# Two-layer hybrid trunk on one core: half of a strided gather moved from ScalarE to GpSimd, a deeper first load queue, new hand orders

## The chip, the cores and the metric

The kernel runs on one core of a Trainium2 chip. The metric is device time in microseconds (us). TensorE (PE) multiplies matrices, VectorE (DVE), ScalarE (ACT) and GpSimd (POOL) work elementwise, and SyncE (SP) issues the DMA loads. Each engine runs its own instructions in program order and waits on semaphores for the others.

## The reference

Two layers over x of 256 tokens by 1024 channels, all float32. Each layer has a token mixing and a feed-forward part, both behind an RMS norm whose scale, shift and gate come from a vector c through `w_mod` (the "modulation"):

```
mod = silu(c) @ w_mod[l] + b_mod[l]                  # 6 x 1024 numbers
h   = rms_norm(x, norm1) * (1 + scale1) + shift1
proj = h @ w_in                                      # u (512) | q (512) | 3 x k,v (768) | gates (24)
y_pool = mean of u over windows of 2, 4, 8, 16 tokens, minus u, times pool_w, per group of 128 channels
k_cmp, v_cmp = silu(flatten(32-token blocks, stride 16) @ cmp_w1) @ cmp_w2      # 15 blocks
y_nsa = gated sum of compressed, selected and sliding-window attention (q, k normed and rotated)
x = x + gate1 * (concat(y_pool, y_nsa) @ w_out)
h2 = rms_norm(x, norm2) * (1 + scale2) + shift2
x = x + gate2 * (relu(h2 @ w_ff1)**2 @ w_ff2)
```

## The kernel before

**Layout and precision.** x stays in on-chip memory transposed, 128 partitions by 8 chunks by 256 tokens. Most products are done as three matmuls of split operands: a value is `hi` (rounded) plus `lo` (the rest), and `mm3` (L269) issues hi·hi, hi·lo and lo·hi (L274 to L276). A few products run in plain float32 (L272, L686).

**The stream of weights.** All weights come as one list of tiles of 512 KB (`stream`, L164 to L190), loaded in list order by SP. `load` (L206) issues loads as long as fewer than six tiles lie between the oldest one in use and the newest. `step` (L220) takes the next tile: a "mod" tile goes to one multiply-accumulate on VectorE (L231), which gives one column of the modulation; any other is split, hi by a cast on ScalarE (L237), lo by a subtraction on VectorE (L238), into five buffers of each kind. `pump` (L242) takes as many tiles as its limits allow. The pool of raw tiles has six buffers; those for hi and lo lie idle while the first 24 tiles pass, since these are used as they come (mod, mod, a for each of eight chunks).

**Stages.** 0 to 46 us: the start and layer 0's first projection, chunk by chunk (L674 to L689: two modulation columns, `modulate` with `mt` L427 and `n` L433, then 12 matmuls L686). 46 to about 134 us: layer 0's token mixing. To 315 us: its feed-forward. 315 to about 427 us: layer 1's token mixing. To 608 us: its feed-forward, then the output.

**The order of the mixing.** Each layer's mixing is written as a string of items (`ORDER`), each the name of a closure with numbers: `b,n,..` and `a,c,h` are pieces of the projection (TensorE), `mod,k` is one normalised chunk (ScalarE h L430, VectorE `mt` L427 and h L431), `nl,n` normalises a finished projection tile (VectorE L641, ScalarE L642), `gather,kv` and `comp` the compression, `psums,g` and `pmix,g` the pooling (GpSimd L590 to L594, VectorE L598), `squares`, `rotate`, `sum`, `turn` the norm and rotation of q and k, `pump,m,n` takes stream tiles. The items are issued in that order, and a scheduler then orders every engine's instructions again; the result stands in the order rows below.

**The compression.** The k and v tiles `kvT` are copied by `gather` (L520) into `tb`, eight copies of 64 partitions by 16 by 15 elements that read every sixteenth token; 64 narrow matmuls `ph` (L533) follow, and the rest of the projection stands behind them on TensorE.

**Rotation.** `squares` (L736) gives sums of squares `ss`, GpSimd raises them to the power -1/2 (`rs`, L751), `rotate` (L753) multiplies the projection in its PSUM bank by the tables (`x` L761, two `z` L764) and by that releases the bank, `rotate_sum` (L766) adds and scales.

**Feed-forward.** In layer 1 the first `EARLY_FF` blocks of 128 features are computed from the chunks before the norm's factor is known; the factor is applied to their results (`act`, L972: b copy L980, r L981), and `TURNS` says how many of the eight chunks are normalised (`modulate`) after each block; the blocks after the early ones read these. `NORM_AT` says at which matmul the two halves of the norm's factor are issued, `WARM` how many dummy matmuls (L307) stand at four places of the start, `MODS` after which tile of layer 0's mixing how many of its mod tiles stand in the stream.

Of the kernel before, what the change touches and what calls it, by code (L numbers as in the profile page):

```python
# [10 lines left out]
F32 = mybir.dt.float32  # L11
F32R = mybir.dt.float32r
# [5 lines left out]
L, D, S, P = 2, 1024, 256, 128  # L18
# [9 lines left out]
WARM = (14, 2, 6, 4)  # L28
# [5 lines left out]
EARLY_FF = (8, 11)  # L34
# [3 lines left out]
NORM_AT = ((1, 2), (2, 7), (1, 2), (1, 6))  # L38

TURNS = ((0, 0, 2, 3, 2, 1, 0, 0, 0, 0), (0, 0, 1, 1, 2, 1, 1, 1, 1, 0))  # L40
# [5 lines left out]
MODS = (0, 0, 2, 5, 0, 2, 2, 5, 4, 0, 0, 1, 1, 2)  # L46

ORDER = (
# [79 lines left out]
def raw(ap):  # L128
    return ap.bitcast(F32)
# [3 lines left out]
def trunk(ctx: ExitStack, tc: tile.TileContext, ins, out):  # L133
# [66 lines left out]
    def source(b):  # L200
        w = ins["w_" + b[0] + ("0" if b[:2] == ("a", 0) else "")]
        for i in b[1:]:
            w = w[i]
        return w, (NA if b[0] == "a" else D)

    def load():  # L206
        nonlocal loaded
        while loaded < min(len(stream), min([used] + held) + N_RAW):
# [940 lines left out]
```

## Time and profile before

| | |
|---|---|
| median of 3 runs | 613.72 us (613.46 to 614.18) |
| the profiled execution | 613.58 us, its span 611.8 us, mean granted TensorE clock 0.994 |
| busy | PE 594.2 us, DVE 469.3, ACT 354.8, POOL 72.4 |
| DMA | 147.5 MB, 241 GB/s over the span |

The span is what the trace covers; the remaining 1.8 us lie around it. Busy times are sums over the whole span, so PE is idle in it for 17.6 us; where they lie is a question for the waits and the windows. A row of a timeline has the start, the duration of that line's run of like instructions, engine, line, tile written and tiles read, the count, and in brackets the idle time of the engine before it with what released it.

### The profile page before, as it was taken

How to read it: one execution, taken by the hardware profiler on the slowest of the kernel's cores; microseconds unless marked ns; L12 is line 12 of the kernel's file. 1: busy time of each engine (PE TensorE's matmuls, PEld its weight loads, DVE VectorE, ACT ScalarE, POOL GpSimd, SP SyncE). 2: the span in 40 equal slices, each digit the busy share in tenths (PEclk: the TensorE clock that was granted, in tenths of full speed). 3: DMA queues.
4: the chain of work that ended last, by engine and by line, in shares of the span. 5: the costliest groups of instructions: out<-in, count | busy, mean ns of one | idle time of the engine just before them, and what ended most of it. 6: DMA issues, size and time to landing. Idle time of an engine off the chain costs nothing.

```text
span 611.8 us, 12176 instructions
## 1 busy us (share of the span) xinstructions
PE 594.2 (97%) x4676; PEld 550.3 (90%) x4676; DVE 469.3 (77%) x870; ACT 354.8 (58%) x781; POOL 72.4 (12%) x94
## 2 busy tenths in 40 slices
PE   8899899999999999999998989999999999999997
PEld 5558767789999999999998978788999999999997
DVE  5769999899999888988876979858996765444440
ACT  3125766478777763443447767866887777433330
POOL 1013630040000000010033640003000000000000
PEclk9999999999999999999998989999999999999999
DMA  8999857965799999998993443233667776666600
GB/s 336 368 386 335 320 186 248 335 215 195 263 363 378 333 332 369 321 366 276 388 359 128 149 139 104 70 100 114 204 222 256 232 234 192 186 204 196 196 30 18
DMA packets 40856, 147.51 MB, mean 241 GB/s; under 512 B 4543, under 2 KB 5725, under 8 KB 40541
## 3 DMA queue, kind: packets, MB, share of 16 engines
q1 hardware_dynamic: 40653, 146.20, 69.3%
q8 instruction: 37, 0.61, 0.4%
q10 hardware_dynamic: 144, 0.52, 0.3%
q14 instruction: 22, 0.18, 0.1%
HBM read 145.66 MB, written 1.05 MB: 240 GB/s over the span
## 4 chain that ended last, share of the span: by engine, by line
PE 80%; DVE 8%; DMA 4%; ACT 4%; POOL 2%; issue 2%; ACTq 0%; DVEq 0%
PE pg L275 10%; PE pg L276 10%; PE pg L274 10%; PE pf L275 10%; PE pf L276 10%; PE pf L274 10%; DMA w<-in_w_mod 3%; PE pb L272 2%; PE pout L272 2%; PE po L898 2%; PE pt L879 2%; DVE w L231 2%; DVE h L443 1%; DVE lo L238 1%; PE pa L686 1%
## 5 line engine op out<-in xcount | busy, mean ns | idle before, releaser
L238 DVE TENSOR_TENSOR lo<-w,hi 128x1024 fp32r<-128x1024 f32 (+1 forms) x154 | 189.4, 1234 | 68.7 <-ACT hi L237 68.1
L237 ACT CAST hi<-w 128x1024 fp32r<-128x1024 f32 (+1 forms) x154 | 160.8, 1049 | 127.7 <-PE pg L275 57.9
L275 PE MATMUL pf<-h,hi 128*128 128x256 f32 (+1 forms) x512 | 145.2, 284 | 1.9 <-DVE h L443 1.9
L274 PE MATMUL pf<-h,hi 128*128 128x256 f32 (+1 forms) x512 | 144.3, 283 | 0.0
L276 PE MATMUL pf<-h,lo 128*128 128x256 f32 (+1 forms) x512 | 144.2, 282 | 0.0
L276 PE MATMUL pg<-a,lo 128*128 128x256 f32 x512 | 144.1, 281 | 0.0
L274 PE MATMUL pg<-a,hi 128*128 128x256 f32 x512 | 143.7, 281 | 0.0
L275 PE MATMUL pg<-a,hi 128*128 128x256 f32 x512 | 143.6, 280 | 0.0
L231 DVE SCALAR_TENSOR_TENSOR w<-w,cb 128x1024 f32<-128x1024 f32 x96 | 119.3, 1249 | 10.7 <-DMA w<-in_w_mod 10.0
L275 PEld LDWEIGHTS pf<-h,hi 128*128 128x128 f32 x512 | 96.8, 189 | 3.4 <-DVE h L443 3.4
L276 PEld LDWEIGHTS pf<-h,lo 128*128 128x128 f32 x512 | 96.9, 189 | 0.0
L274 PEld LDWEIGHTS pg<-a,hi 128*128 128x128 f32 x512 | 96.7, 189 | 0.0
L274 PEld LDWEIGHTS pf<-h,hi 128*128 128x128 f32 x512 | 96.5, 189 | 0.1
L275 PEld LDWEIGHTS pg<-a,hi 128*128 128x128 f32 x512 | 96.3, 188 | 0.0
L276 PEld LDWEIGHTS pg<-a,lo 128*128 128x128 f32 x512 | 96.2, 188 | 0.0
L686 PE MATMUL pa<-w,n 128*128 128x280 f32 (+2 forms) x96 | 29.8, 463 | 2.9 <-ACT n L433 2.5
L686 PEld LDWEIGHTS pa<-w,n 128*128 128x128 f32 x96 | 17.7, 190 | 15.0 <-issue 8.3
L274 PE MATMUL pout<-h,hi 128*128 128x256 f32 x96 | 28.0, 296 | 0.4 <-DVE xT L930 0.4
L856 ACT ACTIVATE p<-sc,nm 128x128 f32<-128x128 f32 (+1 forms) x64 | 26.1, 423 | 2.8 <-DVE nm L852 2.3
L985 ACT ACTIVATE r<-r 128x256 f32<-128x256 f32 x64 | 26.3, 415 | 1.4
L1038 DVE SCALAR_TENSOR_TENSOR xT<-pg,mod,xT 128x256 f32<-128x256 f32 x16 | 7.7, 484 | 25.1 <-PE pg L276 25.1
L989 DVE TENSOR_TENSOR a<-r,a 128x256 fp32r<-128x256 f32 x64 | 26.6, 420 | 0.5 <-ACT a L986 0.5
(195 smaller groups left out, 936.6 us busy)
## 6 DMA issues: line engine op xcount, KB each, us to landing
w<-in_w_ff SPq DMA_DIRECT2D x128, 512.0 KB, 4.5
w<-in_w_mod SPq DMA_DIRECT2D x96, 512.0 KB, 5.3
w<-in_w_a SPq DMA_DIRECT2D x16, 524.0 KB, 6.6
w<-in_w_out SPq DMA_DIRECT2D x16, 512.0 KB, 4.3
w<-in_w_b SPq DMA_DIRECT2D x12, 512.0 KB, 6.0
lw<-in_lw SPq DMA_DIRECT2D x2, 1360.0 KB, 9.8
out<-xT SPq DMA_DIRECT2D x8, 128.0 KB, 2.8
late<-in_late SPq DMA_DIRECT2D x1, 899.0 KB, 8.2
```

What stands on the lines that cost most here:

```text
L231: V.scalar_tensor_tensor(w[:, :D], w[:, :D], 1.0, cb, op0=ALU.mult, op1=ALU.mult, accum_out=mod[:, b[1], b[2]:b[2] + 1])
L237: A.copy(hi[:, :n], w[:, :n])
L238: (G if by_pool(*b) else V).tensor_tensor(lo[:, :n], w[:, :n], raw(hi[:, :n]), op=ALU.subtract)
L272: T.matmul(o, lhs[0], rhs[0], start=start, stop=stop)
L274: T.matmul(o, lhs[0], rhs[0], start=start, stop=False)
L275: T.matmul(o, lhs[0], rhs[1], start=False, stop=False)
L276: T.matmul(o, lhs[1], rhs[0], start=False, stop=stop)
L686: T.matmul(pa[t, g][:, :n], N1[:, k, t * P:(t + 1) * P], w[:, c0:c0 + n], start=k == 0, stop=k == KD - 1)
L856: A.activation(p[:, e, b], sc[:, e, b], AF.Exp, bias=nm[:, e, b:b + 1], accum_out=self.sums[:, hd, b:b + 1])
L879: T.transpose(pt[:, c * P:(c + 1) * P], p[:, c * P:(c + 1) * P], ident)
L985: A.activation(w, w, AF.Square)
L989: V.tensor_tensor(aT[1][:, f], ws.pop(f), raw(aT[0][:, f]), op=ALU.subtract)
```

## The change

1. In layer 1, `gather` of the second half (kv = 1) goes to GpSimd: four of its eight copies.
2. The first 24 loads may lie in sixteen buffers: six raw, five hi, five lo. From the 25th on the six raw ones serve as before.
3. Both `ORDER` strings are new. Layer 1's has a new item `warm,3` (three dummy matmuls) ahead of `mod,7`. Some flags that say whether ScalarE or VectorE does a scaling differ.
4. `WARM`, `EARLY_FF`, `NORM_AT`, `TURNS` and `MODS` have new numbers.

```diff
-WARM = (14, 2, 6, 4)
+WARM = (14, 1, 9, 2)
-EARLY_FF = (8, 11)
+EARLY_FF = (8, 9)
-NORM_AT = ((1, 2), (2, 7), (1, 2), (1, 6))
+NORM_AT = ((1, 3), (2, 7), (0, 5), (1, 6))
-TURNS = ((0, 0, 2, 3, 2, 1, 0, 0, 0, 0), (0, 0, 1, 1, 2, 1, 1, 1, 1, 0))
+TURNS = ((0, 0, 2, 3, 2, 1, 0, 0, 0, 0), (0, 0, 0, 1, 3, 1, 0, 0, 3, 0))
-MODS = (0, 0, 2, 5, 0, 2, 2, 5, 4, 0, 0, 1, 1, 2)
+MODS = (0, 0, 2, 5, 0, 2, 2, 5, 6, 0, 0, 1, 0, 1)
...
-    "pump,0,2 tables norm,0 b,4,0,7 b,4,7,8 pump,1,4 b,5,0,7 b,5,7,8 keep,5 keep,4 norm,1 mod,0 nl,4 nl,5 b,3,0,8 "
+    "pump,1,1 tables b,4,0,7 pump,2,5 norm,0 b,4,7,8 b,5,0,7 b,5,7,8 keep,4 norm,1 keep,5 nl,4 nl,5 pump,2,4 "
...
+    homes, slots, n_first = {}, {}, 3 * KD
+    for i in range(len(stream)):
+        r = i % (N_RAW + 2 * N_SPLIT)
+        homes[i] = "raw" if i >= n_first or r < N_RAW else "hi" if r < N_RAW + N_SPLIT else "lo"
+        slots.setdefault(homes[i], []).append(i)
+
+    def room(i):
+
+        at = slots[homes[i]]
+        n = at.index(i) - (N_RAW if homes[i] == "raw" else N_SPLIT)
+        return n < 0 or at[n] < used and at[n] not in held
...
-        while loaded < min(len(stream), min([used] + held) + N_RAW):
+        while loaded < len(stream) and room(loaded):
...
-            tiles[loaded] = wraw.tile([P, NA], F32, tag="raw", name="w")
+            if homes[loaded] == "raw":
+                tiles[loaded] = wraw.tile([P, NA], F32, tag="raw", name="w")
+            else:
+                tiles[loaded] = raw(wsp.tile([P, NA], F32R, tag=homes[loaded], name=homes[loaded]))
...
-                        A.copy(tb[par * HD:(par + 1) * HD, :, kv, 15 * g:15 * g + 15], src)
+                        to = tb[par * HD:(par + 1) * HD, :, kv, 15 * g:15 * g + 15]
+                        if kv and not first:
+                            G.tensor_copy(to, src)
+                        else:
+                            A.copy(to, src)
```

In the changed kernel the lines behind `ORDER` are one higher, those behind `load` 17 and those behind `gather` 21 higher than before: L237 is L254, L238 is L255, L430 is L447, L525 is L544 (GpSimd) and L546 (ScalarE), L642 is L663, L750 is L771, L761 is L782, L764 is L785, L769 is L790.

**The gather on ScalarE, layer 1, before.** `rb` is the norm's factor, `kvT` the k and v tiles, `tb` the gathered ones, `u` the pooling input.

```order
L400 COPY rb<-pr 128x256
L237 CAST hi<-w 128x1048
L430 ACTIVATE h_1247<-mt,mod 128x256
L642 ACTIVATE kvT<-nl,early 128x256 x2
L525 COPY tb<-kvT 64x16x15 x8
L642 ACTIVATE u<-nl,bsh 128x256
L430 ACTIVATE h_1247<-mt,mod 128x256
L237 CAST hi<-w 128x1048 x2
```

**The same place after.**

```order
L417 COPY rb<-pr 128x256
L254 CAST hi<-w 128x1048
L663 ACTIVATE kvT<-nl,early 128x256 x2
L447 ACTIVATE h_1258<-mt,mod 128x256
L546 COPY tb<-kvT 64x16x15 x4
L254 CAST hi<-w 128x1048
L663 ACTIVATE u<-nl,bsh 128x256
L447 ACTIVATE h_1258<-mt,mod 128x256
L254 CAST hi<-w 128x1048
```

Four of the eight copies are gone from this row; one h now stands behind `kvT` instead of ahead of it, and the cast that followed `u` and an h stands ahead of them.

**GpSimd at that place, after.** `win` are the pooling sums, made from `u`.

```order
L576 TENSOR_TENSOR ck<-cmpc 30x128
L406 TENSOR_TENSOR r<-v,mhalf 128x2
L544 COPY tb<-kvT 64x16x15 x4
L611 TENSOR_TENSOR win<-u 128x271
L611 TENSOR_TENSOR win<-win 128x269
```

The four copies stand where, before, `win<-u` followed `r` directly.

**Rotation on VectorE, layer 1, before.** `x` and `z` read a projection bank `pa`; the second row of two `z` ends the use of the half bank; `ss` is the sum of squares for GpSimd.

```order
L238 TENSOR_TENSOR lo<-w,hi 128x1048 x2
L761 TENSOR_TENSOR x<-pa,ca 128x256
L750 TENSOR_SCALAR ss<-ss 128x4
L764 TENSOR_TENSOR z<-pa,sb 128x4x32 x2
L761 TENSOR_TENSOR x<-pa,ca 128x256
```

**The same place after**, from the first rotation of the layer on.

```order
L782 TENSOR_TENSOR x<-pa,ca 128x256
L785 TENSOR_TENSOR z<-pa,sb 128x4x32 x2
L255 TENSOR_TENSOR lo<-w,hi 128x1048
L790 TENSOR_TENSOR x<-x,z 128x256
L782 TENSOR_TENSOR x<-pa,ca 128x256
L785 TENSOR_TENSOR z<-pa,sb 128x4x32
L255 TENSOR_TENSOR lo<-w,hi 128x1048
L785 TENSOR_TENSOR z<-pa,sb 128x4x32
L790 TENSOR_TENSOR x<-x,z 128x256
L771 TENSOR_SCALAR ss<-ss 128x4
L782 TENSOR_TENSOR x<-pa,ca 128x256
L785 TENSOR_TENSOR z<-pa,sb 128x4x32 x2
```

Before, `ss` stood between the second rotation's `x` and its two `z`. After, both `z` of that rotation stand ahead of this `ss`, with one weight split between them, and the third rotation stands behind it.

## Rows read from the trace of the kernel before

**Rows 1.** the longest waits of TensorE: line, releaser, us in total, times, longest

```profile
PE pa L274 <- DVE z L764: 2.8, 1, 2.8
PE pa L686 <- ACT n L433: 2.5, 3, 1.3
PE pf L275 <- DVE h L443: 1.9, 6, 0.7
PE ph L533 <- ACT tb L525: 1.6, 1, 1.6
```

**Rows 2.** layer-1 mixing by 15 us: length, busy per engine, PEclk, DMA share, GB/s

```profile
330.00:345.00 15.00, 15.00 (x155) 14.43 (x156) 14.09 (x27) 10.84 (x23) 9.00 (x12) 0.89 0.33 107
345.00:360.00 15.00, 12.21 (x91) 11.39 (x90) 11.73 (x31) 8.49 (x40) 11.10 (x11) 0.98 0.43 141
360.00:375.00 15.00, 14.90 (x113) 14.02 (x113) 13.72 (x40) 11.40 (x40) 3.39 (x3) 0.91 0.42 129
```

**Rows 3.** chain from 8 to 46 us: start, duration, what

```profile
18.13 7.46 DMA w<-in_w_mod
```

**Rows 4.** three 15 us windows of layer 0

```profile
15.00:30.00 15.00, 13.42 (x46) 8.15 (x45) 10.76 (x25) 2.03 (x4) 0.00 (x0) 1.00 1.00 373
60.00:75.00 15.00, 13.94 (x139) 11.19 (x138) 13.72 (x37) 11.30 (x54) 9.32 (x13) 1.00 0.88 327
120.00:135.00 15.00, 13.59 (x108) 12.75 (x106) 14.77 (x26) 9.84 (x20) 6.74 (x7) 1.00 0.66 234
```

**Rows 5.** page part 5, the layer-0 projection: busy, mean ns, idle before

```profile
L686 PE MATMUL pa<-w,n 128*128 128x280 f32 (+2 forms) x96 | 29.8, 463 | 2.9 <-ACT n L433 2.5
```

**Rows 6.** ScalarE in order of time: start, us, instruction, [idle <-releaser]

```profile
324.32 0.90 ACT L642 ACTIVATE kvT<-nl,early 128x256 f32<-128x256 f32 x2
325.12 4.83 ACT L525 COPY tb<-kvT 64x240 f32<-64x240 f32 x8
...
355.55 1.06 ACT L772 ACTIVATE x<-x,rs 128x64 f32<-128x64 f32 x4 [3.65 <-POOL rs L751]
```

**Rows 7.** TensorE, the compression matmuls of layer 0 and of layer 1

```profile
61.92 2.06 PE L533 MATMUL ph<-tb,lw 128*64 128x31 f32 x64
...
330.00 2.06 PE L533 MATMUL ph<-tb,lw 128*64 128x31 f32 x64 [1.58 <-ACT tb L525]
```

**Rows 8.** line L371, the GpSimd plain copies: duration ns min/median/max

```profile
L371 POOL COPY sumssq<-sq x3: 412/734/922, 124.4 to 417.5; 128x256 f32<-128x256 f32 x3
```

**Rows 9.** GpSimd in order of time

```profile
330.62 0.64 POOL L590 TENSOR_TENSOR win<-u 128x271 f32<-128x271 f32 x1 [10.16 <-ACT u L642]
...
349.95 1.01 POOL L751 TENSOR_TENSOR rs<-ss,mhalf 128x4 f32<-128x4 f32 x1
...
352.07 3.44 POOL L751 TENSOR_TENSOR rs<-ss,mhalf 128x4 f32<-128x4 f32 x1
```

**Rows 10.** VectorE in order of time

```profile
324.15 1.24 DVE L238 TENSOR_TENSOR lo<-w,hi 128x1048 fp32r<-128x1048 f32 x1
...
352.25 2.39 DVE L238 TENSOR_TENSOR lo<-w,hi 128x1048 fp32r<-128x1048 f32 x2
...
357.51 0.17 DVE L750 TENSOR_SCALAR ss<-ss 128x4 f32<-128x4 f32 x1 [2.54 <-ACT z L745]
357.59 0.48 DVE L764 TENSOR_TENSOR z<-pa,sb 128x128 f32<-128x128 f32 x2
```

**Rows 11.** TensorE, keep-warm matmuls at the start

```profile
12.02 1.03 PE L307 MATMUL idle<-diagb 128*128 128x512 bf16 x4
```

**Rows 12.** VectorE in the layer-1 feed-forward

```profile
429.45 0.16 DVE L980 COPY b<-pf 128x1 f32<-128x1 f32 x1 [0.53 <-PE pf L276]
...
449.61 0.15 DVE L980 COPY b<-pf 128x1 f32<-128x1 f32 x1
...
451.53 0.47 DVE L431 SCALAR_TENSOR_TENSOR h<-mt,mod,h 128x256 fp32r<-128x256 f32 x1
```

**Rows 13.** a 15 us window of the layer-1 feed-forward

```profile
435.00:450.00 15.00, 15.00 (x127) 15.00 (x126) 14.92 (x34) 13.67 (x26) 0.00 (x0) 1.00 0.64 199
```

49 rows, old and new, of the table ORDER are left out of this document.

## Prediction

> **What bounds the kernel now.** I read the page's busy shares first: TensorE is busy for 594.2 of 611.8 us, so every gain has to come from its 17.6 us of idle time or from its clock. Second the list of TensorE's waits [rows 1]: four of them make up 8.8 us, namely 2.8 us for VectorE's second `z` of a rotation, 2.5 us in layer 0's first projection, 1.9 us where layer 0's feed-forward begins, and 1.6 us for the last of the eight `tb` copies. Third the windows of layer 1's mixing [rows 2]: there the clock column is not 1.00 but 0.89, 0.98 and 0.91. That is worth 15 x 0.11 = 1.65 us after the first of the two waits (it comes behind the wait for `tb` and the 2.06 us of narrow matmuls, [rows 7]) and 15 x (0.02 + 0.09) = 1.65 us after the second. Each of these two waits is thus paid about twice. The two feed-forwards have nothing to give: in [rows 13] TensorE is busy 15.00 of 15 us.
>
> So four places decide: the first projection, the end of layer 0's mixing, the gather of layer 1, the rotation of layer 1. The rest is what the new order puts in.
>
> **Part 1, the first 24 loads through sixteen buffers.** The chain through this stage [rows 3] waits longest for a load of a modulation tile, 7.46 us from issue to landing, and goes on over VectorE, ScalarE and TensorE. TensorE works 29.8 us here and waits 2.5 us for `n` [rows 5]; more than 2.5 us can't be won. Issuing earlier helps only if the DMA engines were short of work; [rows 4] shows their share at 1.00 from 15 to 30 us at 373 GB/s, with six buffers. A deeper queue can only let fifteen engines go on where one is late. I take half of the wait: -1.3 (0 to -2.5). The dummy matmuls of the start are 0.26 us each [rows 11] and stand where TensorE waits for other things; the two sums of `WARM` are both 26, so 0.
>
> **Part 2, layer 0's mixing.** TensorE's order there is nearly the old one. What can shrink is the 1.41 us of idle time in the window 120 to 135 us [rows 4], part of the 1.9 us for `h` [rows 1]: two modulation tiles stand earlier in the stream, so the output weights' splits are less crowded. What can grow is a wait the shuffle puts in; its nearest row is the 1.6 us of `ph`. I take -0.5 (-1.9 to +1.6).
>
> **Part 3, the gather.** ScalarE's eight copies start at 325.12 and take 4.83 us, 0.60 each [rows 6]; `ph` starts at 330.00 and TensorE had been ready 1.58 us before, at 328.42 [rows 7]. With four copies and one h (0.5 us) ahead of them, as the order rows show, ScalarE is done near 325.2 + 2.4 = 327.6, before TensorE asks. GpSimd decides. It idles from about 320.5 to 330.62 [rows 9], so its four can start when `kvT` is there, near 324.9. No row has this copy on GpSimd. The nearest are its plain copies of 128 x 256, 0.41 to 0.92 us with median 0.73 [rows 8]; four at 0.73 end at 327.8.
>
> To that comes what VectorE does to it. GpSimd's `rs` of 128 x 4 takes 1.01 us at 349.95 and 3.44 us at 352.07 [rows 9], and beside the second one two subtractions run on VectorE for 2.39 us [rows 10]: the difference, 2.43, is just their length. So I let GpSimd stand still while VectorE runs operations of this kind. Behind 324.9 VectorE has the rest of one `lo` (of 1.24 us, [rows 10]), one h and one `mt`, together about 1.4 us, before its next `lo` waits for ScalarE's cast behind the copies. That gives 329.2, a wait of 0.8; where GpSimd gets in between, less. I take a wait of 0.6, so -1.0 of the 1.58 (bounds: -1.6 with 0.41 each and no blocking; +1.0 with copies that are slower on strided data, below).
>
> The Trainium skill, "SBUF — State Buffer", section "Who interferes with whom", says that an operation of VectorE with two inputs in this memory holds the read port shared with GpSimd and that the other one blocks fully. By that rule the 2.43 us above is what it should be, and the trace agrees; without the rule the wait would be 0 and the sum 0.6 less.
>
> The clock behind it: 1.65 us are lost now. The wait shrinks from 1.6 to 0.6 us, but the narrow matmuls stay. Both ends are open, 0 and -1.65; I take -1.0.
>
> **Part 4, what layer 1's order adds.** Three dummy matmuls at 0.26 [rows 11]: +0.7 (0 if they fall into a wait, +0.8). The pooling `win` chain starts after the copies on GpSimd, and VectorE's first pooling scaling now stands ahead of five of the eight h of the projection chunks; if it waits, everything behind it on VectorE does, and TensorE waits for the last h. I take +0.7 (0 to +1.8, the time of a `lo` and an h that follow it, 1.24 + 0.5).
>
> **Part 5, the rotation.** TensorE's 2.8 us end with the two `z` at 357.59, released by `ss` in front of them, for which VectorE had idled 2.54 us [rows 10]. The chain is: GpSimd's long `rs` ends 355.51 [rows 9], ScalarE had waited 3.65 us for it [rows 6], then computes the squares for this `ss`. After, the order rows show both `z` of this rotation ahead of `ss`. Without `ss`, `z` could have run right behind `x`, near 355, and released the bank at 355.5; TensorE wanted it at 355.42. The `lo` between the two `z` may cost some. The stall's place is taken by the third rotation, which now stands behind `ss`, but TensorE needs that bank one piece of the projection later. I take a wait of 0.6: -2.2 (0 to -2.8). Its clock follow-up: -1.2 of 1.65 (0 to -1.65).
>
> **Part 6, layer 1's feed-forward.** A block takes 24 matmuls, 24 x 15/127 = 2.83 us [rows 13]. The first block's result is read at 429.45 right when TensorE is done, so the ninth ends at 429.45 + 8 x 2.83 = 452.1 and, with nine early blocks, the next one wants the last chunk 7/8 of a block later, at 454.6. The last chunk is normalised in the pass behind the ninth block's copy; a pass of this kind takes from 449.61 to the end of h at 452.00, 2.4 us [rows 12], so it is ready at 454.5. No slack: +0.2 (0 to +1.2, one weight split ahead).
>
> **Sum.** -1.3 - 0.5 - 1.0 - 1.0 + 0.7 + 0.7 - 2.2 - 1.2 + 0.2 = -5.6. The profiled execution took 613.58 us (611.8 in the span, 1.8 around it), 0.14 below the median, so the forecast is 613.72 - 5.6 = 608.1 us. Its own range is 605.3 to 611.0.
>
> **Rivals.**
> (a) *The clock does not come back.* The narrow matmuls alone, or a rest of the waits, let the clock fall as before. For it: the drop behind `ph` follows 2.06 us of matmuls of 31 columns, which stay. Against it: layer 0 has the same matmuls at 61.92 [rows 7], and the clock of that window is 1.00 [rows 4]. The two clock terms are 0: 608.1 + 2.2 = 610.3 us. The Trainium skill, "TensorE: Matmul & The Clock Gate", ties the clock to recent activity; this trace agrees in that both drops follow an idle stretch, and doesn't tell idle time from narrow matmuls.
> (b) *Strided copies are slow on GpSimd.* The same number of microseconds for fewer elements is what ScalarE shows: 240 strided ones take 0.60, so a penalty is likely somewhere. At 0.73 x 1.6 = 1.17 us each and 1.4 blocked they end at 331.0: `ph` 1.0 later than now instead of 1.0 sooner (+2.0), no clock (+1.0), and VectorE's scaling waits fully (+1.1): 612.2 us.
> (c) *Nothing moves.* As (b), and the first projection keeps its wait, because the DMA engines were full before: 612.2 + 1.3 = 613.5 us.
> (d) *Slower: GpSimd's copies are stretched as `rs` was.* Place: `tb` in layer 1. If each of the four takes the 2.4 us extra of that row, 3.1 each, they end at 324.9 + 12.5 = 337.4, 8.2 us later than I assume, and the clock term goes: 608.1 + 8.2 + 1.0 = 617.3 us. It decides from where the copies' end eats the whole gain: 5.6 - 1.0 = 4.6 us behind 329.2, so from 2.2 us a copy. For it: no copy with this stride has run on GpSimd in this trace. Against it: VectorE has only some 1.4 us of blocking work there, and then waits itself.
>
> **How the numbers follow.** Chances: the forecast 0.55, (a) 0.14, (b) 0.12, (c) 0.10, (d) 0.09. Within 0.2% (1.2 us, about what a measurement of this kernel can tell from no change) is 612.5 to 614.9. The forecast, (a) and (b) lie below it: faster 0.81. (c) lies in it, with nothing of the others: same 0.10. (d) is above it: slower 0.09. The range leaves out (d), and the half of (c) that is nearest to no change, and a little at the low end, where both clock terms, the whole first wait and all of part 5 would come (608.1 - 1.2 - 0.6 - 0.65 - 0.6 - 0.45 = 604.6): 604.4 to 613.2.
>
> **What would show it.** Part 1: TensorE's wait for `n` below 1.3 us, the last of its chunks done near 44.4 instead of 45.7. Part 3: four copies on GpSimd of 0.6 to 1.1 us, ended before 329.5, `ph` waiting under 1 us, the clock of the 15 us behind it above 0.93. Part 5: no wait over 1 us for `z`, the clock there above 0.95. Part 4: a new wait of a projection matmul for h, under 2 us. Part 6: none of the feed-forward matmuls waits over 1 us for h. The forecast is wrong if the copies take over 2 us, if a wait over 2 us appears elsewhere in layer 1's mixing, or if the first projection becomes longer.

## The result: 604.64 us, and the profile after

The changed kernel takes 604.64 us (median of 4 runs, 604.45 to 604.70) against 613.95 us for the kernel before beside it (4 runs, 613.46 to 614.20). The ratio is 0.985, 95% interval 0.9835 to 0.9866: faster by 9.3 us. The forecast was 608.1 us with a range of 604.4 to 613.2; the time lies just inside the range, and below the forecast's own range (605.3 to 611.0).

TensorE's waits of the changed kernel, to be read beside [rows 1] (line, releaser, us in total, times, longest):

```profile
PE pa L707 <- ACT n L450: 1.4, 2, 0.7
PE pf L292 <- DVE h L460: 1.4, 4, 0.7
PE pout L291 <- DVE xT L951: 1.2, 2, 0.9
PE pa L293 <- DVE h L448: 1.1, 1, 1.1
...
PE pt L900 <- ACT pcT L839: 0.8, 1, 0.8
```

Two of the four long waits are gone, that for `tb` and that for `z`. The first projection waits 1.4 us instead of 2.5. New are 1.1 us of a projection matmul for VectorE's h, 0.8 us for a copy of the attention, and 0.9 us of the output projection of layer 1; that of layer 0 now waits 0.3 us, before 1.0.

The windows of layer 1's mixing, beside [rows 2] (the changed kernel is 4 us earlier at the start of this mixing and 9 us at its end; PEclk is the third number from the end):

```profile
315.00:330.00 15.00, 15.00 (x173) 14.82 (x173) 10.72 (x20) 11.90 (x25) 8.94 (x15) 1.00 0.56 199
330.00:345.00 15.00, 13.86 (x103) 12.43 (x103) 14.97 (x38) 8.07 (x18) 10.49 (x15) 1.00 0.45 138
345.00:360.00 15.00, 15.00 (x121) 14.67 (x120) 14.96 (x42) 10.84 (x44) 5.37 (x6) 1.00 0.55 171
360.00:375.00 15.00, 14.16 (x119) 11.54 (x118) 14.55 (x40) 14.03 (x63) 0.00 (x0) 1.00 0.26 80
```

The clock is 1.00 in all four, where it was 0.89, 0.98 and 0.91.

Where the 9.3 us came from is easiest to see by stages. A stage here ends with the start of the first matmul of the next one, read from each kernel's trace:

| stage | before, us | after, us | difference |
|---|---|---|---|
| start and first projection (to the first `pb`) | 45.58 | 43.54 | -2.04 |
| layer 0's mixing (to the first `pf`) | 80.41 | 78.88 | -1.53 |
| layer 0's feed-forward (to layer 1's first `pb`) | 189.62 | 189.09 | -0.53 |
| layer 1's mixing, to `ph` | 14.39 | 12.97 | -1.42 |
| from `ph` to the first `pa` | 10.25 | 8.78 | -1.47 |
| from there to layer 1's first `pf` | 77.99 | 75.60 | -2.39 |
| layer 1's feed-forward and the end | 193.55 | 193.67 | +0.12 |
| span | 611.8 | 602.5 | -9.3 |

Each column is one profiled execution. How far a stage moves from one execution to the next can be seen where kernels share it. Layer 0's mixing took 80.41, 80.46, 80.22, 80.95 and 79.56 us in five profiles that have the old one with the old load rule (before, gpool, rot3, bwarm, l1), and 78.87 to 79.40 us in five that have the new one with the deep queue. A microsecond in this stage is thus within the scatter of the old kernel; the two groups don't meet.

The gather after the change, GpSimd and ScalarE (beside [rows 6] and [rows 9]) and the matmuls behind it (beside [rows 7]):

```profile
321.05 3.18 POOL L544 COPY tb<-kvT 64x240 f32<-64x240 f32 x4 [4.33 <-ACT kvT L663]
325.44 1.23 POOL L611 TENSOR_TENSOR win<-u 128x271 f32<-128x271 f32 x1 [1.22 <-ACT u L663]
```

```profile
320.07 0.91 ACT L663 ACTIVATE kvT<-nl,early 128x256 f32<-128x256 f32 x2
320.88 0.50 ACT L447 ACTIVATE h<-mt,mod 128x256 fp32r<-128x256 f32 x1
321.29 2.51 ACT L546 COPY tb<-kvT 64x240 f32<-64x240 f32 x4
```

```profile
324.48 2.06 PE L554 MATMUL ph<-tb,lw 128*64 128x31 f32 x64
```

GpSimd's four copies end at 324.23 and ScalarE's four at 323.80, and `ph` starts at 324.48 without a wait in brackets. The two halves are balanced to 0.4 us.

The rotation, beside [rows 10]: VectorE's second and third rotation, and ScalarE and GpSimd before it.

```profile
345.37 1.26 DVE L255 TENSOR_TENSOR lo<-w,hi 128x1048 fp32r<-128x1048 f32 x1
...
347.23 0.27 DVE L785 TENSOR_TENSOR z<-pa,sb 128x128 f32<-128x128 f32 x1
347.42 1.23 DVE L255 TENSOR_TENSOR lo<-w,hi 128x1048 fp32r<-128x1048 f32 x1
348.58 0.28 DVE L785 TENSOR_TENSOR z<-pa,sb 128x128 f32<-128x128 f32 x1
...
349.24 0.16 DVE L771 TENSOR_SCALAR ss<-ss 128x4 f32<-128x4 f32 x1
...
349.64 0.48 DVE L785 TENSOR_TENSOR z<-pa,sb 128x128 f32<-128x128 f32 x2
```

```profile
344.34 2.00 POOL L772 TENSOR_TENSOR rs<-ss,mhalf 128x4 f32<-128x4 f32 x2
```

Both halves of the second rotation's `z` now end before `ss` at 349.24, and VectorE has no idle time in front of any of these rows. GpSimd's two `rs` take 1.0 us each, where one of them had taken 3.44.

### The profile page after: what moved, and what is told of

Same layout as the page of the kernel before. It is cut to its first block, busy times and chain, and to the rows that moved or that the text cites. A ratio compares the mean times of both kernels' runs of the same rounds, so it can differ in the third digit from the quotient of the medians.

```text
span 602.5 us, 12181 instructions
## 1 busy us (share of the span) xinstructions
PE 590.4 (98%) x4679; PEld 547.4 (91%) x4679; DVE 466.7 (77%) x864; ACT 354.5 (59%) x796; POOL 71.7 (12%) x98
## 4 chain that ended last, share of the span: by engine, by line
PE 83%; DVE 8%; DMA 4%; ACT 2%; POOL 1%; issue 1%; SPq 0%; DVEq 0%; ACTq 0%; POOLq 0%
PE pg L293 10%; PE pg L292 10%; PE pf L292 10%; PE pg L291 10%; PE pf L293 10%; PE pf L291 10%; PE pa L707 3%; PE pout L289 2%; PE pb L289 2%; PE po L919 2%; DMA lo<-in_w_mod 2%; DVE lo L255 2%; PE pt L900 2%; DMA w<-in_w_a 1%; PE pout L291 1%; DVE h L460 1%
## 5 line engine op out<-in xcount | busy, mean ns | idle before, releaser
L255 DVE TENSOR_TENSOR lo<-w,hi 128x1024 fp32r<-128x1024 f32 (+1 forms) x154 | 188.3, 1226 | 67.0 <-ACT hi L254 66.3
L254 ACT CAST hi<-w 128x1024 fp32r<-128x1024 f32 (+1 forms) x154 | 161.0, 1049 | 120.4 <-PE pg L292 59.6
L248 DVE SCALAR_TENSOR_TENSOR w<-w,cb 128x1024 f32<-128x1024 f32 x88 | 109.8, 1255 | 6.3 <-DMA w<-in_w_mod 5.7
L291 PE MATMUL pout<-h,hi 128*128 128x256 f32 x96 | 27.9, 297 | 1.2 <-DVE xT L951 1.2
L292 PE MATMUL pout<-h,hi 128*128 128x256 f32 x96 | 26.9, 282 | 0.0
L293 PE MATMUL pout<-h,lo 128*128 128x256 f32 x96 | 26.9, 281 | 0.0
```

Of the source, the lines that this page charges most:

```text
L248: V.scalar_tensor_tensor(w[:, :D], w[:, :D], 1.0, cb, op0=ALU.mult, op1=ALU.mult, accum_out=mod[:, b[1], b[2]:b[2] + 1])
L254: A.copy(hi[:, :n], w[:, :n])
L255: (G if by_pool(*b) else V).tensor_tensor(lo[:, :n], w[:, :n], raw(hi[:, :n]), op=ALU.subtract)
L291: T.matmul(o, lhs[0], rhs[0], start=start, stop=False)
L292: T.matmul(o, lhs[0], rhs[1], start=False, stop=False)
L293: T.matmul(o, lhs[1], rhs[0], start=False, stop=stop)
```

## Experiments

Each was timed beside the kernel before on the same chip. There the kernel before spread further than in the first comparison (613.92 us, 611.53 to 615.63 in the 13 runs beside the first four experiments). Much of that lies in the first stage: it took 44.71 to 47.43 us in the eight profiles with the old load rule. So results are read by the stages of the profiled run as much as by the total. TensorE's mean granted clock over a run is on record for every run and tells the runs with a stretch of low clock from those without.

### The queue alone (q_only)

```diff
 # the kernel before
-        while loaded < min(len(stream), min([used] + held) + N_RAW):
+        while loaded < len(stream) and room(loaded):
...
```

> The kernel before with the deeper first load queue alone. Theory 1 (the queue's gain is its own: with sixteen buffers the other DMA engines go on while one is late): -2.0 us (-1.5 to -2.5), all of it before 46 us, the first layer-0 output projection matmul pb near 43.6 instead of 45.6, GB/s from 15 to 45 us near 405 instead of 375. Theory 2 (the new order or the modulation tiles moved in the stream give it): within 0.5 us of before, pb still near 45.6.

Measured: 610.96 us (610.83 to 611.40), ratio 0.9948 (0.9934 to 0.9963), -3.0 us by the medians; the first `pb` starts at 43.67, 1.91 us earlier, and layer 0's mixing takes 79.76 instead of 80.41. A window of its first stage (length, busy per engine, clock, DMA share, GB/s):

```profile
15.00:30.00 15.00, 15.00 (x52) 9.56 (x51) 11.63 (x29) 2.03 (x4) 0.00 (x0) 1.00 1.02 410
```

The DMA engines moved 410 GB/s where [rows 4] has 373, at nearly the same busy share (1.02 and 1.00). Theory 1 holds for the stage: in all six profiles with the deep queue it took 43.38 to 43.77 us, in the eight without it 44.71 to 47.43. The total is half a microsecond beyond its range. Layer 0's mixing was 0.65 us shorter, which was not expected; that is within the scatter named above.

### The old load rule in the changed kernel (no_q)

```diff
 # the changed kernel
-        while loaded < len(stream) and room(loaded):
+        while loaded < min(len(stream), min([used] + held) + N_RAW):
...
```

> The changed kernel with the old load rule (six raw buffers from the start). Theory 1 (the queue's gain is its own and goes on a little into layer 0's mixing, as the run with the queue alone showed: 1.9 us before 46 us, 0.65 after): +2.6 us over the changed kernel's 604.6 (+2 to +3.2), pb at 45.6. Theory 2 (the new order and the moved modulation tiles would hide it): under +1. In both, layer 0's mixing keeps what the order and the tiles bring, 78.9 + 0.65 = 79.5 us instead of 80.4.

Measured: 607.82 us (605.92 to 608.88), ratio 0.9901 (0.9867 to 0.9934) to the kernel before, where the changed kernel has 0.985: +3.2 us by the medians; `pb` at 45.54, layer 0's mixing 79.41 us. Theory 1, with a wider spread: the four runs differ by 3.0 us, those of the changed kernel by 0.25. The clock was up (0.999 or 1.000) in all four.

### The moved modulation tiles alone, and with layer 0's order (mods, l0)

```diff
 # mods: the kernel before
-MODS = (0, 0, 2, 5, 0, 2, 2, 5, 4, 0, 0, 1, 1, 2)
+MODS = (0, 0, 2, 5, 0, 2, 2, 5, 6, 0, 0, 1, 0, 1)
 # l0: the same, and layer 0's ORDER string of the changed kernel
...
```

> The kernel before with the moved modulation tiles alone (two of them earlier in layer 0's stream). Theory 1 (the tiles bring the gain, since TensorE's wait for h at the start of the feed-forward stands behind VectorE's work on them): the stage 79.6 us and the waits for h 1.4 instead of 1.9, -0.8 to -1.2. Theory 2 (the new order brings it): stage 80.2 to 80.6, within 0.4 us of before.

> The kernel before with the new order of layer 0's mixing and the moved modulation tiles, nothing else. Theory 1 (these two bring what the run without the deep queue kept in layer 0): the stage from the first pb to the first layer-0 feed-forward matmul is 79.4 us instead of 80.4 and the feed-forward 0.4 shorter, so -1.4 us in all. Theory 2 (they only help with early loads): within 0.4 us of before.

Measured: 613.62 and 613.49 us, ratios 1.0001 and 1.0002 (both 0.9982 to 1.0021). Neither theory as a whole. The stage was shorter, as theory 1 of both said: 79.54 us with the tiles alone (-0.9), 79.39 us with the order too (-1.0), instead of 80.41. That this is the tiles' work is not shown: l1, which has neither the tiles nor the new order of layer 0, took 79.56 us. And the feed-forward did not get shorter, the waits for h stayed at 2.0 us, and in these two profiled runs layer 1's mixing was longer by as much: 103.86 and 103.54 us instead of 102.63. Whether 0.9 us are left in the total can't be told, since the interval of 0.2% is 1.2 us to either side. TensorE's longest wait in the run with the tiles alone:

```profile
PE pa L274 <- DVE z L764: 3.5, 1, 3.5
```

The wait for `z` has grown from 2.8 to 3.5 us. `ph` waited for `tb` as long as before (1.6 us), but this time the clock did not fall behind it:

```profile
330.00:345.00 15.00, 14.36 (x160) 13.61 (x161) 14.07 (x27) 11.05 (x23) 9.60 (x13) 1.00 0.35 107
345.00:360.00 15.00, 11.49 (x81) 10.66 (x80) 11.73 (x31) 8.49 (x40) 11.18 (x11) 0.92 0.43 141
360.00:375.00 15.00, 15.00 (x110) 14.23 (x109) 12.64 (x36) 10.26 (x35) 3.40 (x3) 0.86 0.37 108
```

TensorE came earlier to the rotation by that and waited longer, since VectorE came no earlier: its `ss` before `z` stands 27.55 us behind `ph` (357.56 and 330.01), in the kernel before 27.51 [rows 7, 10]. Behind the longer wait the clock lost 15 x (0.08 + 0.14) = 3.3 us, where it was 1.65. That the moved tiles have to do with this is not shown: layer 1 is the same in both kernels, and rot3, which has no moved tiles, has no drop behind `ph` either.

It does show what the first drop was worth in the old order. From `ph` to the first `pa` it is 10.25 and 10.20 us with the drop (before, q_only) and 9.59 to 9.60 without (mods, l0, rot3). Of the 1.65 us of lost clock 0.65 was gained there; in mods and l0 that came back as the longer wait for `z`.

### Layer 1's order and the GpSimd copies alone (l1)

```diff
 # the kernel before
-    "pump,0,2 tables norm,0 b,4,0,7 b,4,7,8 pump,1,4 ...
+    "pump,1,1 tables b,4,0,7 pump,2,5 norm,0 b,4,7,8 ...
...
+                        if kv and not first:
+                            G.tensor_copy(to, src)
```

> The kernel before with the new order of layer 1's mixing and its four copies on GpSimd, nothing else. Theory 1 (the parts add): layer 1's mixing, from its first pb to its first feed-forward matmul, 97.4 us instead of 102.6, -5.3 us in all, clock 1.00 throughout. Theory 2 (part of it needs the earlier loads of layer 0 or the new feed-forward numbers): -3.5 or less.

Measured: 608.10 us (607.00 to 608.96), ratio 0.991 (0.9884 to 0.9935), -5.7 us by the medians; the mixing of layer 1 took 97.25 us. Theory 1: this part needs nothing from the others. Its first stage took 47.43 us in the profiled run, 1.9 us longer than before, which is the old load rule's spread again. Layer 0's feed-forward took 189.25 us here, so 0.4 of the 0.5 us by which it is shorter in the changed kernel come with layer 1's order string. (That stage scatters little: 189.60 to 189.63 us in before, gpool, rot3 and bwarm.) By the medians q_only, l0 and l1 add up to -3.0 - 0.3 - 5.7 = -8.9 us, close to the -9.3 of the whole.

### Four copies on GpSimd with the old order (gpool)

```diff
 # the kernel before
-                        A.copy(tb[par * HD:(par + 1) * HD, :, kv, 15 * g:15 * g + 15], src)
+                        if kv and not first:
+                            G.tensor_copy(to, src)
+                        else:
+                            A.copy(to, src)
```

> The kernel before with four of the eight tb copies of layer 1 on GpSimd and the old order strings. Theory 1 (the wait for tb and the clock after it are paid by ScalarE's eight copies): ph 1.4 us earlier without a wait, the clock of the 15 us behind it 1.00 instead of 0.89, so -1.4 - 1.65 = -3.0 us (-2.4 to -3.3). Theory 2 (the new order is what makes it work; VectorE's queue takes the wait's place): -1.4 at ph given back by a wait for h before the next projection, total -1 to 0. Theory 3 (the narrow matmuls alone let the clock fall): -1.4, clock still 0.89.

Measured: 611.24 us (610.09 to 612.75), ratio 0.9955 (0.9937 to 0.9973), -2.7 us. The wait for `tb` is gone and the clock is 1.00. Layer 1's mixing took 99.16 us, 3.5 less. That is the size of theory 1, but not its path: only 0.4 us came between `ph` and the first `pa`, where theory 1 has the clock's 1.65, and 1.4 us behind it. Theory 2's new waits exist as well, 1.6 us of `tqk` for h and 0.9 us of `py` for `win`; TensorE's list for `tqk` and for `z`:

```profile
PE tqk L786 <- DVE h L612: 1.6, 1, 1.6
...
PE pa L274 <- DVE z L768: 0.6, 1, 0.6
```

What was not expected is that the long wait for `z` is down to 0.6 us. VectorE's row shows why: the order strings are the old ones, but the scheduler has put both `z` of the second rotation ahead of `ss` here, as in the changed kernel.

```profile
352.91 1.24 DVE L238 TENSOR_TENSOR lo<-w,hi 128x1048 fp32r<-128x1048 f32 x1
354.07 0.47 DVE L768 TENSOR_TENSOR z<-pa,sb 128x128 f32<-128x128 f32 x2
...
356.04 0.16 DVE L754 TENSOR_SCALAR ss<-ss 128x4 f32<-128x4 f32 x1
```

GpSimd's `rs` took 2.12 and 1.19 us here, not 1.01 and 3.44, so `ss` could come sooner too. It still starts at 356.04, and TensorE wanted the bank at 354.09. In the kernel before TensorE went on 0.70 us behind the start of `ss` (358.21 and 357.51); with that order it would have gone on near 356.74 here, a wait of some 2.6 us (an estimate from these rows) instead of 0.6. So the order removed most of the wait.

### The first scaling later (rot3)

```diff
 # the kernel before, layer 1
-    ... a,0,0 sum,0,2,1,1 gexp,0,2 ... pump,1,1 rotate,0,0,1 ...
+    ... a,0,0 gexp,0,2 ... sum,0,2,1,1 pump,2,1 pump,1,1 rotate,0,0,1 ...
```

> The kernel before with one item of layer 1's order, the scaling of the first rotated q (sum,0,2), issued later, behind the rotation of the next ones, so that ScalarE's row no longer has it ahead of the squares that VectorE's ss waits for. Theory 1 (the 2.8 us wait of TensorE for z comes from ScalarE standing behind GpSimd's long rs): the wait is under 0.5 us and the clock behind it 1.00, so -2.5 - 1.65 = -4 us (-3 to -4.5). Theory 2 (VectorE is late there by its own work, the idle 2.5 us would be filled): wait still over 2 us, time within 0.6 us of before.

The item belongs to the keys, not to a q as the expectation says, and by this edit the keys of the first 128 tokens are used before their second half of the rotation is added and before they are scaled. Measured: 609.96 us (608.99 to 612.77), ratio 0.9938 (0.9920 to 0.9956), -4.0 us by the medians. The wait for `z` is gone from TensorE's list, and the mixing of layer 1 took 99.16 us. `ss` still stands between `x` and `z`, but VectorE no longer waits for it, because ScalarE now computes the squares before it waits for `rs`:

```profile
353.20 0.40 DVE L761 TENSOR_TENSOR x<-pa,ca 128x256 f32<-128x256 f32 x1
353.53 0.15 DVE L750 TENSOR_SCALAR ss<-ss 128x4 f32<-128x4 f32 x1
353.60 0.47 DVE L764 TENSOR_TENSOR z<-pa,sb 128x128 f32<-128x128 f32 x2
```

That is theory 1, with two flaws. The keys' use no longer waits for the scaling, which is a second thing that the edit changes. And behind `ph`, which still waited 1.6 us for `tb`, the clock did not fall in this run, so part of the gain is not the edit's. Over the eight runs the clock was 0.997 in three (610.13 to 612.77 us) and at least 0.999 in five (608.99 to 609.97).

### Dummies in the waits for tb (bwarm, gact, gactw)

```diff
 # bwarm: the kernel before, layer 1
-    ... nl,2 mod,2 comp ...
+    ... nl,2 mod,2 warm,6 comp ...
 # gact: the changed kernel
-                        if kv and not first:
+                        if kv and not first and False:
 # gactw: gact, layer 1
-    ... nl,2 pump,2,2 pump,1,4 comp ...
+    ... nl,2 pump,2,2 pump,1,4 warm,8 comp ...
```

> The kernel before with six dummy matmuls of 512 columns ahead of the narrow ph matmuls of layer 1, in the 1.58 us in which TensorE waits for tb. Theory 1 (the clock falls because TensorE stood still): no low clock from 332 to 336, ph at the same time, so -1.6 us (-1.2 to -1.7). Theory 2 (it falls because of the 2.06 us of narrow matmuls): clock as before, time within 0.3 us of before.

> The changed kernel with all eight tb copies of layer 1 on ScalarE again. Theory 1 (GpSimd's share is needed): the copies end near 326.7, ph 2.2 us later than 324.5, the clock behind it open, +2.2 to +3.9 us. Theory 2 (VectorE's row sets the end of this stage, so TensorE would only wait less later): +0.3 to +1.2.

> The changed kernel with all eight copies on ScalarE, and eight dummy matmuls of 512 columns in the 2.1 us in which TensorE then waits for tb. Beside the same kernel without the dummies (609.3, span 607.4, clock 0.89 and 0.88 in the two 15 us windows about ph). Theory 1 (standing still makes the clock fall): both windows 1.00, 3.4 us of low clock saved, of which later waits on VectorE may take up to 1.5, so 606 to 607.5. Theory 2 (the narrow matmuls make it fall): clock as without, 609 to 609.6.

Measured: bwarm 612.12 us (611.29 to 613.09), ratio 0.9971 (0.9949 to 0.9993), -1.8 us with the clock at 1.00 (at least 0.999 in all five runs), as theory 1. The path is not theory 1's: from `ph` to the first `pa` only 0.3 us were gained, since 1.0 us of `py` for GpSimd came in. Behind it the wait for `z` fell from 2.8 to 0.4 us, because the scheduler has both `z` ahead of `ss` here too, and a new wait of 1.6 us for `tqk` took part of that back.

gact 609.32 us (607.89 to 609.76), +4.7 us over the changed kernel, more than theory 1's upper end. The wait and the windows of it, and the windows of gactw:

```profile
PE ph L554 <- ACT tb L546: 2.1, 1, 2.1
```

```profile
315.00:330.00 15.00, 12.86 (x141) 12.66 (x139) 7.78 (x16) 12.24 (x21) 5.27 (x11) 0.89 0.48 170
330.00:345.00 15.00, 15.00 (x114) 14.11 (x113) 13.25 (x27) 8.16 (x19) 5.97 (x9) 0.88 0.48 142
```

```profile
315.00:330.00 15.00, 14.59 (x164) 13.29 (x163) 7.94 (x16) 12.62 (x22) 5.26 (x11) 1.00 0.49 180
330.00:345.00 15.00, 14.33 (x108) 12.90 (x107) 14.28 (x35) 9.49 (x25) 7.57 (x14) 1.00 0.44 142
```

In gact 15 x (0.11 + 0.12) = 3.45 us of clock went in the profiled run. gactw took 607.24 us (606.65 to 607.72), 2.1 us less, with the same copies, the same narrow matmuls and `ph` 0.16 us earlier: theory 1. With dummies in the wait the clock was at least 0.999 in all four runs; the narrow matmuls do not lower it. Without them it did not fall each time: gact's clock was 0.994 in three runs (609.32 to 609.76 us) and 1.000 in two (607.89 and 608.09). So the drop costs gact some 1.4 us of time, less than the 3.45 us of lost clock, and gact without a drop is still 3.3 us slower than the changed kernel.

### All eight copies on GpSimd (gall)

```diff
 # the changed kernel
-                        if kv and not first:
+                        if not first:
```

> The changed kernel with all eight tb copies of layer 1 on GpSimd. At 0.80 us each (the mean of the four) they end near 321.05 + 6.4 = 327.4, ph 2.9 us later. Theory 1 (the halves are balanced, more on either engine costs): +2.9 us, and the pooling sums behind the copies start 2 us later, so up to +4.5. Theory 2 (ScalarE, relieved of its four, brings the casts and VectorE's row forward and gives it back): +1 to +2.

Measured: 609.64 us (609.09 to 609.71), +5.0 us. `ph` waited 3.1 us for GpSimd, the stage to `ph` took 16.17 us (+3.2), and the clock fell behind it (0.98 and 0.91: 1.65 us; the mean clock was 0.997 in this run and 0.994 in the other four). Theory 1. Of the splits tried four and four is the best: all eight on either engine cost 4.7 to 5.0 us, of which 2.2 and 3.2 us are the later `ph`.

### Without the three dummies (nowarm)

```diff
 # the changed kernel, layer 1
-    ... pmix,3 mod,4 pump,1,5 warm,3 mod,7 comp ...
+    ... pmix,3 mod,4 pump,1,5 mod,7 comp ...
```

> The changed kernel without the three dummy matmuls in layer 1. Theory 1 (they are paid where TensorE has no wait of its own, but it waits 1.1 us for VectorE's h six us later, and that wait would grow by their 0.8): within 0.5 us of the changed kernel, clock 1.00. Theory 2 (they keep the clock): clock under 1.00 behind 333 us, +0.8 to +1.6 us. Theory 3 (they cost what they take): -0.8 us.

Measured: 605.54 us (605.16 to 607.73), +0.9 us.

```profile
PE pa L293 <- DVE h L448: 1.8, 1, 1.8
```

```profile
330.00:345.00 15.00, 13.22 (x88) 11.85 (x88) 14.39 (x35) 8.15 (x19) 9.64 (x15) 0.89 0.48 141
```

These rows are from the slowest of the four runs, 607.73 us, the only one with a lower clock (0.997). In it the wait for h has grown (1.1 to 1.8 us) and the clock fell behind it, as theory 2 says. In the other three (605.16 to 605.75 us) the clock was at least 0.999, which is theory 1, at 0.5 to 1.1 us over the changed kernel. So the dummies cost nothing, since no run without them was faster. That they keep the clock is shown by one run in four against none in the four of the changed kernel, which is thin. Their removal also let the scheduler order some of VectorE's later rows differently, so the 0.9 us is not the dummies' alone.

## Why the prediction was right, and where its terms were too small

**The sign and the places were right, the size was not.** Two of the four waits named went, the two others became shorter, and no term had the wrong sign. All terms of gain were too small, which is why the sum of -5.6 became -9.3; the time lies only 0.24 us inside the stated range. By stages: the first projection -2.0 (forecast -1.3), layer 0's mixing -1.5 (-0.5), its feed-forward -0.5 (nothing), layer 1's mixing -5.3 (-4.0), the rest +0.1 (+0.2).

**Part 1, the first loads: -1.3, measured -2.0.** The mis-sized step is "I take half of the wait". The first `pa` starts at 13.4 us in both kernels, as the unchanged sum of `WARM` said. Behind it TensorE waited 2.6 us before, 2.3 for `n` and 0.3 for a load; 0.7 us are left, and 1.1 in q_only. (The list's 1.4 us contain 0.7 us ahead of the first `pa`; that is why the sign "below 1.3" was missed.) The reason for taking half was the share of 1.00: "Issuing earlier helps only if the DMA engines were short of work". With more loads in the queue the rate rose from 373 to 410 GB/s at nearly the same share, so a share of 1.00 was no proof of the highest rate.

**Part 2, layer 0's mixing: -0.5, measured -1.5.** Which edit brings it is open. mods and l0 have 79.54 and 79.39 us, q_only 79.76, each within the 79.56 to 80.95 of the old stage or 0.2 us below it; only together, in the five profiles with tiles, order and deep queue (78.87 to 79.40), is the stage clearly shorter. The place was wrong. The prediction read the 1.9 us for `h` [rows 1] as the start of layer 0's feed-forward; by time only 1.1 us of them lie there, and these stay. (In the window from 100 to 150 us TensorE's list has `pf` waiting for h three times, 1.1 us together, before and after.) The other 0.8 us lie at the start of layer 1's feed-forward, where 0.3 us are left. Nor did the end of layer 0's mixing change: the window 120 to 135 has 13.57 us of TensorE now and 13.59 in [rows 4]. The idle time that went lies earlier: from 75 to 90 and from 105 to 120 us TensorE is busy 14.98 and 15.00 us now, 14.27 and 14.24 before. Gone from there are 0.5 of a wait of 0.7 us of `py` for `win` and 0.8 us of the output projection.

**Part 3, the gather: -1.0, measured -1.4.** The copy on GpSimd takes 0.62 to 0.97 us, mean 0.76 (0.80 with the gaps), against 0.73 taken and 1.4 us of blocking on top. Its four copies took 3.18 us in all, where 4 x 0.73 and the blocking would be 4.3. The blocking by `lo`, h and `mt` that the prediction assumed is there, but it is worth some 0.6 us (3.06 us for the four copies against 4 x 0.62), not 1.4; the last section shows the rows. Rivals (b) and (d), strided or stretched copies, are refuted by 0.62 to 0.97 us each; that holds for four copies beside the VectorE work of this place. The clock term -1.0 was -1.65 by the window: with no wait there was no drop, and gactw shows that the narrow matmuls had no part in it. Rival (a) falls. The stage from `ph` to the first `pa` became 1.47 us shorter, and by mods, l0 and rot3 only 0.65 of that is what the absent drop alone gives; the rest is the new order's.

**Part 4: +0.7 and +0.7, measured +0.8 and +1.1.** The wait for h is there, 1.14 us ahead of the matmul at 339.19. The three dummies are 0.81 us of TensorE's time. In nowarm this wait is 1.8 us without them, so most of their time would be waited anyway.

**Part 5: -2.2 and -1.2, measured -2.8 and -1.65.** The wait is gone whole, the clock too. The chain that the prediction reads, long `rs`, ScalarE's scaling, its squares, `ss`, `z`, is the right one, and the runs cut it in two places. rot3 takes the scaling out of it and keeps `ss` ahead of `z`: no wait. gpool and bwarm, like the changed kernel, have both `z` ahead of `ss`: 0.6 and 0.4 us are left. Where neither was cut (before, q_only, mods, l0) the wait is 2.8 to 3.5 us. In the changed kernel, gpool and bwarm the long `rs` went as well; what that alone would give in the changed kernel was not separated.

**Part 6: +0.2, measured +0.12 for the stage.** The last chunk's h ends as computed, 2.4 us behind the ninth block's copy, and no matmul waits for it: the copy starts at 442.45 and h ends at 444.86. The small sum hides two items that the prediction did not have: the waits for h at the stage's start fell by 0.5 us, and the output projection of layer 1 now waits 0.9 us. The numbers of the feed-forward were not run alone.

**Rival (c)**, that a full DMA keeps the first wait, falls with part 1.

Layer 1's mixing can be checked by TensorE's own account: the waits for `tb` and `z`, -1.6 and -2.8, the lost clock, -3.3, the new wait for h, +1.1, the dummies, +0.8, and the longer wait for the attention's copy, which the prediction did not have, +0.7, give -5.1; measured are -5.3.

## What to carry to other kernels

A wait of the matmul engine can cost more than its length: in the profiled run of this kernel two waits of 4.4 us together were followed by 3.3 us of lost clock. So price both, but give the clock a range. The same program kept its clock in some runs and lost it in others (gact 2 of 5, nowarm 3 of 4), and time won back from the clock was in part waited again a few microseconds later (bwarm, mods). One profiled run does not tell which case is the usual one; the clock on record for every run does. When a wait is unavoidable and over a microsecond, dummy matmuls inside it cost nothing here (bwarm, gactw).

Look up at which time a wait lies before you build on its sum: the 1.9 us for `h` were two places, and the larger one did not change. And when an edit removes a wait that it was not aimed at, read the engine's row again: gpool changed no order string and bwarm only put dummies in, and the scheduler moved `z` ahead of `ss` all the same.

## What the runs showed of the hardware

**The clock after a wait.** Beside each other, in the profiled runs of layer 1's mixing: no drop after 1.1 us (changed kernel) and after two waits of 1.6 us for `tqk` (bwarm, gpool); after the same 1.6 us for `tb` a drop in the kernel before and in q_only and none in mods, l0 and rot3; a drop after 1.8 (nowarm), 2.1 (gact), 2.8 (before), 2.9 (q_only), 3.1 (gall) and 3.5 us (mods, l0). A profile shows one run only, and the drop is not the same in each: by the mean clock there was none in two of five runs of gact, in three of four of nowarm, and in two of the last 21 of the kernel before. Why the same wait is sometimes followed by a drop and sometimes not is open. The Trainium skill, "TensorE: Matmul & The Clock Gate", section "What's actually happening", ties the clock to recent activity; these runs agree in that each drop here begins in a wait or behind one, and gactw adds that the narrow matmuls did not lower the clock.

**GpSimd beside VectorE.** The same `rs` of 128 x 4 takes 1.01 us in most places, 2.12 us beside one `lo` that started with it (gpool), and 3.44 us beside two (before, and again in q_only, mods and l0). Each long one ends 0.87 or 0.88 us behind the `lo` that held it: the `lo` end at 354.64 (before) and 350.80 (gpool), the `rs` at 355.51 and 351.68. The four copies show the same. In the changed kernel the first three end 0.45 or 0.46 us behind the VectorE instruction that was running when they began, `lo` (321.56), h (322.31) and `mt` (323.10); the fourth had none beside it and took 0.62 us. In gall two copies began in the middle of a `lo` and a third began just ahead of one:

```profile
320.82 1.38 POOL L544 COPY tb<-kvT 64x240 f32<-64x240 f32 x1 [3.93 <-ACT kvT L663]
...
323.00 0.75 POOL L544 COPY tb<-kvT 64x240 f32<-64x240 f32 x1
...
323.78 1.52 POOL L544 COPY tb<-kvT 64x240 f32<-64x240 f32 x1
```

```profile
320.50 1.24 DVE L255 TENSOR_TENSOR lo<-w,hi 128x1048 fp32r<-128x1048 f32 x1
321.66 0.83 DVE L448 SCALAR_TENSOR_TENSOR h<-mt,mod,h 128x256 fp32r<-128x256 f32 x1
...
323.20 1.65 DVE L255 TENSOR_TENSOR lo<-w,hi 128x1048 fp32r<-128x1048 f32 x1
```

The first and the last end 0.45 or 0.46 us behind their `lo`. The middle one, which began ahead of the `lo` at 323.20, was not held by it; that `lo` took 1.65 us instead of 1.24, and the h behind a copy takes 0.83 us instead of 0.48 (gact, where no copy runs on GpSimd there). So each engine holds the other up, and it matters which began first: the second `rs` of the changed kernel began at 345.33, 0.04 us ahead of a `lo`, and took 1.01 us. The Trainium skill, "SBUF — State Buffer", section "Who interferes with whom", has the rule that a VectorE instruction with two inputs in this memory contends with a GpSimd one that reads it, and that issue order decides who blocks; these rows agree.

**Load depth and spread.** With six buffers the kernel's time spread by 3 to 4.5 us from run to run (before 611.23 to 615.77 in the last 21 runs, no_q 605.92 to 608.88); with sixteen for the first 24 loads the spread was 0.25 us in the changed kernel and 0.6 in q_only. The larger spreads of gact (1.9 us) and nowarm (2.6) go with the clock: among runs with the same clock they are 0.2 to 0.6 us. The 1.1 us of gactw, with the clock up in all four runs, are not explained.
